# Memory keys and values from plain float32 products, the gating table loaded first, and a new recorded order, in a two-layer encoder trunk on one core

## The chip, the core and the metric

One core of one Trainium2 chip runs the whole program. The metric is the device time of one execution in microseconds; the kernel before has a median of 1061.03 us over three runs (1059.38 to 1061.39). One further execution was taken by the hardware profiler. Every duration below that is not called a median comes from that one.

The engines are named as in the profile: PE (TensorE, matrix products), DVE (VectorE), ACT (ScalarE), POOL (GpSimd), and SP, which issues nearly all the DMAs.

## What is computed

Two layers over a residual stream of 256 tokens by 1024 channels. Each layer is a half-weighted gated feed-forward network, a mixer with an output projection, and a second gated network, with a layer normalization after each. The mixer of layer 0 is a recurrence over time (RWKV-7), that of layer 1 a stick-breaking attention; both also attend to 256 fixed memory tokens, whose keys and values are projected once:

```python
mem_kv = mem @ w_mem_kv                      # (256 x 1024) @ (1024 x 512)
mem_k = split_heads(mem_kv[..., :MEM_WIDTH])
mem_v = split_heads(mem_kv[..., MEM_WIDTH:])
for i in range(DEPTH):
    x = layer_norm(ALPHA * x + 0.5 * swiglu(x, ffn1_w_gate[i], ffn1_w_up[i], ffn1_w_down[i]), ...)
    proj = x @ (rwkv_w_in if i % 2 == 0 else sb_w_in)
    mix = rwkv7_mix(...) or stick_breaking_mix(...)
    heads = concatenate([mix, memory_attention(mq, mem_k, mem_v)])
    x = layer_norm(ALPHA * x + heads @ w_out[i], ...)
    x = layer_norm(ALPHA * x + 0.5 * swiglu(x, ffn2_w_gate[i], ffn2_w_up[i], ffn2_w_down[i]), ...)
```

All arrays are float32. `swiglu` is `(silu(x @ gate) * (x @ up)) @ down`.

## The kernel before

**Tiles.** The 256 tokens are two halves of 128 rows (`hf` 0 and 1). A feed-forward network runs over eleven blocks of 256 hidden channels. For one block and half, PE makes gate and up together (512 columns, eight steps over the 1024 channels), ACT and DVE form the gated product, PE turns it, and PE adds the down products into two accumulation banks of that half.

**Parts.** Most products are not made in float32. A weight piece of 128 x 1024 is loaded into a `raw` buffer; ACT rounds it into `hi` (type float32r) and DVE subtracts, giving the remainder `lo` (`piece`). The moving operand is split in the same way (`split_T`, from a turned tile in PSUM into `xTh`/`xTl` or a `hT` pair), and `mm3` issues three products: hi by hi, hi by lo, lo by hi. The rings hold 11 `raw`, 9 `hi` and 8 `lo` buffers. Where a block is named in `WHOLE`, its down products are plain float32 products of the loaded weights instead, one instruction for three, without ACT and DVE work on the weights.

**Memory.** `memory_kv` loads the two halves of the memory, turns them by PE in two groups of four 128-column blocks, splits each turned group into parts (`mT`, in one `hi` and one `lo` buffer), loads `w_mem_kv` in four pieces of 512 KB, splits each, and makes 8 x 2 x 3 = 48 products of 512 columns into two banks. `mem_attention` reads the results.

**Layer order in time.** The mixer of half 0 runs beside the first network's blocks of half 1; that of half 1 runs beside the second network's blocks of half 0. What follows the last network is the normalization of half 1 and the output. In layer 0 the mixer's end is a chain of small products of 64 x 64 (`Tt`, `Y`, `T`, `L`, `Lm`, `vn`, `Sk`, `S` and so on are its tiles) with DVE and ACT steps between them. This document calls the stretch from its first product out of `Tt` and `Lm` to the first large product after the memory attention the chain; it runs once for each half.

**Tables.** ACT holds one set of function tables. A change of set (Exp, Sigmoid, Ln, Silu; Tanh is in three of them) is one ACT_TABLE_LOAD. `TANH` names blocks whose Silu is made from a Tanh, so that no change is needed, by one more DVE instruction.

**What sets the order.** The program first records every operation as an `Op` in a `Plan`, with a price from `Plan.price`. `Plan.order` then lays them out one by one: of the operations that could start earliest on an engine it takes the one with the smallest priority `pri` (with a charge for a change of table). `Plan.improve` finds the priorities by 60 rounds of backward passes with random shakes and then by 76 seeds (`MOVES`) that shift the priorities of a stretch. On each engine the instructions run in the order laid out; PE, ACT and DVE queues are in order, so an instruction that waits holds up all behind it.

Every operation is issued from one line of `Plan.issue`, so all rows of the profile carry line L636, and a row is told apart by its tiles. A buffer keeps the name of its first user: `raw_20r` is a `raw` buffer whatever it holds, `idle_1r` and `h_33r` hold gated products, `ps_28r` and `ps_29r` are the banks of gate, up and projections, `ps_4r` and `ps_5r` those of turned tiles.

Of the kernel before, what the change touches and what calls it, by code (L numbers as in the profile page):

```python
# [13 lines left out]
F32 = mybir.dt.float32  # L14
F32R = mybir.dt.float32r
I32 = mybir.dt.int32
AF = mybir.ActivationFunctionType
# [4 lines left out]
P = 128  # L22
# [36 lines left out]
TANH = (((0, 1, 2, 3, 4, 8, 9), (1, 2, 3, 5, 9)), ((0, 1, 2, 3, 8, 9), (0, 1, 8)))  # L59
WHOLE = (((1, 2, 4, 5, 6, 9, 10), (0, 1, 2, 4, 5, 6, 7)), ((3,), (1, 6)))  # L60
# [9 lines left out]
ORDERS = ((3, 1, 2, 0), (1, 0, 2, 3), (1, 3, 0, 2), (3, 0, 1, 2))  # L70
FLAGS = dict(t1=False, bt=False, dc=False, out1=False, zl2=False)
# [45 lines left out]
class Engine_:  # L117
# [12 lines left out]
ROUNDS = 60  # L130
SHAKES = (0.0, 100.0, 300.0)
PATIENCE = 8
MOVES = (
# [6 lines left out]
)  # L140
SEED = 5104
TURN = 47040.0


def moved(pri, seed, engines):

    r = random.Random(seed)
    a, width = r.uniform(-2e3, 1.055e6), r.choice((4e3, 1e4, 2e4, 4e4, 1e5))
    sigma, only = r.choice((100.0, 400.0, 1500.0, 4000.0)), r.choice((None, None, None, "PE", "DVE", "ACT", "SP"))
    part, new = r.choice((1.0, 0.3, 0.1, 0.03)), list(pri)  # L150
    for i, x in enumerate(pri):
        if a <= x < a + width and (only is None or engines[i] == only) and r.random() < part:
            new[i] = x + r.gauss(0.0, sigma)
    return new


class Plan:
# [159 lines left out]
    def price(self, o, method, aps, a, k):  # L317
# [11 lines left out]
        elif o.eng == "PE":  # L329
# [4 lines left out]
            if method == "transpose":  # L334
                took, o.lag = 110.0, 175.0
            elif st.dtype == F32R:
                took, o.lag = max(cols / 2.4, m / 1.2) + 13.3, 180.0
            else:
                took, o.lag = 2 * max(cols / 1.2, m / 1.2 + 4), 200.0
                if rows <= 64 and cols > 128:  # L340
                    took *= 1.25
            o.parts.append((took, [(r, c) for r in half(st, rows) for c in half(out, m)], min(rows, P) / P))
        elif o.eng == "ACT":
# [3 lines left out]
            o.took = 95.0 + 0.845 * n + far + 93.0 * ptr + (92.0 if "accum_out" in k else 0.0)  # L347
            o.lag = 95.0
        elif o.eng == "DVE":
# [6 lines left out]
            if sum(free(x) == 1 for x in ins) > 2:  # L356
                o.took += 115.0
# [210 lines left out]
    def improve(self):  # L568

        rng = random.Random(SEED)  # L570
        engines, self.first = [o.eng for o in self.ops], dict(self.groups)
# [3 lines left out]
        for n in range(ROUNDS):  # L575
# [12 lines left out]
            if last[-1] < best[-1]:  # L588
                best, kept, fails = last, (dict(self.buffer), self.groups, last[-2]), 0
                pri = [o.pri for o in self.ops]  # L590
# [4 lines left out]
        if MOVES:  # L595
            for seed in MOVES:
                pri = moved(pri, seed, engines)
            for o in self.ops:
                o.pri = pri[o.i]
            key = lambda i: pri[self.lead[i]] - 4000.0 if i in self.lead else pri[i]  # L600
            self.groups = {k: sorted(g, key=key) for k, g in self.first.items()}
            best = self.order()
            kept = dict(self.buffer), self.groups, best[-2]
# [36 lines left out]
def kernel(ctx, tc, const, x, mem, f1g, f1u, f1d, f2g, f2u, f2d, ln_g, ln_b, w_out, w_mem_kv,  # L640
# [31 lines left out]
    def piece(shape, *srcs, queue=None):  # L672
# [242 lines left out]
    def memory_kv():  # L915
# [5 lines left out]
        for g in range(2):  # L921
# [87 lines left out]
    def rwkv_constants():  # L1009
# [19 lines left out]
        nc.gpsimd.memset(lastc, 0.0)  # L1029
        R.update(gup=gup, rkb=rkb, S=S, lastc=lastc)  # L1030

    def rwkv(hf, res):
# [12 lines left out]
        def shifted(c0, n, *dests):  # L1045

            ch = c0 // P
            ptv = turned(project(hf, rw_in[0], c0, n), 0, n // P)
# [63 lines left out]
        zv = sl("vn", [P, NT, P])  # L1112
        shifted(768, 512, zk[:, 0:4])
        shifted(1280, 512, zk[:, 4:6], zv[:, 0:2])
# [50 lines left out]
        shifted(1792, 512, zv[:, 2:6])  # L1165
# [29 lines left out]
        v = zv.rearrange("p j t -> p (j t)")  # L1195
        V = hv(v)
        hb = hv(sl("g"))
        for g in range(2):
# [78 lines left out]
        for x, view in enumerate(("p i j -> p j i", "p i j -> p i j")):  # L1277
            xv = v4(Xs[x], False)
            nc.copy(xv[:, :, 0:BLK], Tn.rearrange(view), lane[:, 0:1])
            nc.copy(xv[:, :, BLK:], Tn.rearrange(view), lane[:, 1:2])  # L1280

        def put_back(x, scratch, dst, crossed):
# [5 lines left out]
            for b in range(2):  # L1288
                src = sv[:, :, b].rearrange("p s h -> p h s")
                for to, ts, hs in parts:  # L1290
# [44 lines left out]
        for lastl in (False, True):  # L1335
# [16 lines left out]
            for x in (0, 1) if not lastl else (1,):  # L1352
                with nc.together():
                    n = products(six((ac, "tp")), T if x else Y, Y if x else T, 1, 1 - x)
# [8 lines left out]
                if x and not lastl:  # L1363
                    for g in range(2):
                        gs = slice(6 * g, 6 * g + 6)
                        nc.vector.tensor_sub(T[:, gs], T[:, gs], keep[g])
# [248 lines left out]
    nc.gpsimd.memset(idle, 0.0)  # L1615
    bank = ps("acc1")
# [71 lines left out]
```

## Time and profile before

| what | value |
|---|---|
| median of three runs | 1061.03 us |
| the profiled execution, its own time | 1062.11 us |
| span of the instructions in it | 1060.3 us |
| PE busy | 1043.7 us, 98% |
| DVE busy | 879.3 us, 83% |
| ACT busy | 748.0 us, 71% |
| ACT_TABLE_LOAD | 19, 1283 ns each |
| moved by DMA | 303.18 MB, mean 286 GB/s |

The profiled execution is 1.1 us above the median of the runs, and 1.8 us of its time lie outside its span. A matrix product's end is modelled, and products overlap, so the busy time of PE is not the sum of what the products cost; the distance between the starts of two products that follow each other is the better price. A plain float32 product stands as two records in the trace, a product of parts or a turned block as one.

### The profile page before, as it was taken

Reading aid. Unit: us, or ns where it says so; the run is one execution under the profiler, and the core shown is the slowest. Engines: PE = TensorE matmul, PEld = TensorE weight load, DVE = VectorE, ACT = ScalarE, POOL = GpSimd, SP = SyncE. Lnnn points to the kernel's source line nnn. Section 1 sums busy time; section 2 is a strip of 40 time slices with the busy share of each in tenths; the row PEclk is TensorE's granted clock in tenths of the full one; section 3 lists DMA queues with packets and bytes.
Section 4 is the critical chain, followed back from the end, with each engine's and each line's share of the span. In section 5 each row is a group of like instructions: output and inputs, shape, how many; then the busy total and the mean of one; then the engine's idle time right before and its main releaser. Section 6 shows DMA issues by size and latency. Waiting matters only on the chain.

```text
span 1060.3 us, 17884 instructions
## 1 busy us (share of the span) xinstructions
PE 1043.7 (98%) x6275; PEld 836.5 (79%) x6275; DVE 879.3 (83%) x1240; ACT 748.0 (71%) x1067; POOL 5.2 (0%) x20
## 2 busy tenths in 40 slices
PE   8999999999899999999999999999999999999996
PEld 7888888876788766778888888888778777878885
DVE  5776679998999978988799755659899989986796
ACT  6665558967789987667577655547997999676672
POOL 0000000000000000000000000000000000000000
PEclk9999999999899999999999999999999999999998
DMA  9998869778598888899899976758989988998981
GB/s 325 324 368 260 257 197 353 243 235 300 187 300 276 270 282 267 299 329 356 293 330 364 327 231 200 232 169 289 368 297 315 365 287 276 372 366 277 307 279 66
DMA packets 212683, 303.18 MB, mean 286 GB/s; under 512 B 13892, under 2 KB 159728, under 8 KB 212594
## 3 DMA queue, kind: packets, MB, share of 16 engines
q1 hardware_dynamic: 212050, 301.53, 85.6%
q8 instruction: 49, 0.80, 0.3%
q10 hardware_dynamic: 544, 0.52, 0.2%
q14 instruction: 40, 0.33, 0.1%
HBM read 300.95 MB, written 1.05 MB: 285 GB/s over the span
## 4 chain that ended last, share of the span: by engine, by line
PE 94%; ACT 3%; DVE 1%; DMA 1%; issue 0%; ACTq 0%; DVEq 0%; SPq 0%
PE ps_28r L636 28%; PE ps_29r L636 28%; PE ps_24r L636 8%; PE ps_26r L636 8%; PE ps_2r L636 8%; PE ps_25r L636 7%; PE ps_4r L636 3%; PE ps_5r L636 3%; ACT T_338r L636 1%; DMA raw_20r<-in_w_mem_kv_dram 1%; DVE x L636 0%; DMA raw_8r<-in_ffn_w_up_dram 0%; ACT Tt_331r L636 0%; ACT hi_18r L636 0%; ACT bn_383r L636 0%
## 5 line engine op out<-in xcount | busy, mean ns | idle before, releaser
L636 ACT ACTIVATE idle_1r<-ps_29r 128x256 f32<-128x256 f32 (+1 forms) x45 | 19.2, 427 | 27.0 <-PE ps_29r L636 22.2
L636 ACT ACTIVATE h_33r<-ps_28r 128x256 f32<-128x256 f32 (+1 forms) x47 | 19.4, 412 | 24.1 <-PE ps_28r L636 22.8
L636 PE MATMUL ps_28r<-lo_13r,xTh 128*128 128x512 f32 x84 | 32.7, 390 | 0.0
L636 PE MATMUL ps_29r<-lo_13r,xTh 128*128 128x512 f32 x76 | 29.6, 390 | 0.0
L636 ACT ACT_TABLE_LOAD x19 | 24.4, 1283 | 5.8 <-DMA raw_8r<-in_ffn_w_up_dram 5.5
L636 PE MATMUL ps_28r<-lo_40r,xTh 128*128 128x512 f32 (+1 forms) x72 | 27.6, 384 | 0.0
L636 PE MATMUL ps_28r<-lo_43r,xTh 128*128 128x512 f32 (+1 forms) x72 | 27.6, 384 | 0.0
L636 PE MATMUL ps_28r<-hi_15r,xTh 128*128 128x512 f32 (+1 forms) x64 | 26.2, 409 | 0.0
L636 PE MATMUL ps_29r<-lo_22r,xTh 128*128 128x512 f32 x64 | 25.0, 390 | 0.0
L636 PE MATMUL ps_28r<-hi_15r,xTl 128*128 128x512 f32 (+1 forms) x64 | 24.6, 384 | 0.0
L636 PE MATMUL ps_28r<-hi_12r,xTh 128*128 128x512 f32 (+1 forms) x60 | 23.8, 396 | 0.0
L636 PE MATMUL ps_29r<-lo_16r,xTh 128*128 128x512 f32 x60 | 23.4, 390 | 0.0
L636 DVE TENSOR_TENSOR h_33r<-h_33r,ps_28r 128x256 f32<-128x256 f32 x32 | 13.3, 416 | 12.1 <-ACT h_33r L636 12.1
L636 PE MATMUL ps_28r<-hi_12r,xTl 128*128 128x512 f32 (+1 forms) x60 | 23.0, 384 | 0.0
L636 PE MATMUL ps_28r<-hi_6r,xTh 128*128 128x512 f32 x52 | 21.1, 406 | 1.5 <-ACT xTh L636 1.5
L636 PE MATMUL ps_29r<-hi_21r,xTh 128*128 128x512 f32 x56 | 22.4, 401 | 0.0
L636 PE MATMUL ps_29r<-hi_39r,xTh 128*128 128x512 f32 x54 | 22.1, 409 | 0.0
L636 PE MATMUL ps_29r<-hi_21r,xTl 128*128 128x512 f32 x56 | 21.9, 390 | 0.0
L636 PE MATMUL ps_29r<-hi_42r,xTh 128*128 128x512 f32 x52 | 21.6, 416 | 0.0
L636 PE MATMUL ps_28r<-hi_18r,xTh 128*128 128x512 f32 x52 | 21.4, 412 | 0.0
L636 PE MATMUL ps_28r<-hi_45r,xTh 128*128 128x512 f32 (+1 forms) x54 | 21.4, 397 | 0.0
L636 PE MATMUL ps_28r<-hi_6r,xTl 128*128 128x512 f32 x52 | 21.0, 404 | 0.2 <-DVE xTl L636 0.2
(2127 smaller groups left out, 3919.0 us busy)
## 6 DMA issues: line engine op xcount, KB each, us to landing
raw_41r<-in_ffn_w_down_dram SPq DMA_DIRECT2D x17, 512.0 KB, 5.4
raw_11r<-in_ffn_w_gate_dram SPq DMA_DIRECT2D x32, 256.0 KB, 4.5
raw_11r<-in_ffn_w_up_dram SPq DMA_DIRECT2D x32, 256.0 KB, 4.4
raw_14r<-in_ffn_w_gate_dram SPq DMA_DIRECT2D x29, 256.0 KB, 5.0
raw_14r<-in_ffn_w_up_dram SPq DMA_DIRECT2D x29, 256.0 KB, 6.1
raw_23r<-in_ffn_w_gate_dram SPq DMA_DIRECT2D x29, 256.0 KB, 4.5
raw_23r<-in_ffn_w_up_dram SPq DMA_DIRECT2D x29, 256.0 KB, 4.9
raw_53r<-in_ffn_w_down_dram SPq DMA_DIRECT2D x14, 512.0 KB, 6.5
```

The costliest lines, as they stand in the source:

```text
L636: fn(*[at(x) for x in a], **{n: at(x) for n, x in k.items()})
```

## The change

`memory_kv` no longer splits anything. The turned memory is copied as it is into a `raw` buffer, each 512 KB piece of `w_mem_kv` stays in its `raw` buffer, and 16 plain float32 products of 512 columns take the place of the 48. A Silu of one column is issued ahead of all other ACT work, on a tile that POOL clears first; the first rounded weight piece comes behind it. Two blocks of layer 1's second network (3 and 4) join `TANH`; the block numbers 8 and 10 that leave or join the other lists belong to blocks that are not issued through those lists. The order in which `w_out` pieces are used for half 0 of layer 1 is another. `Plan.price` prices ACT, DVE and products a little differently. The search in `improve` is replaced by a stored priority for every operation (`URGENCY`, 147 lines of text that are unpacked into numbers). The flags `pb`, `xt`, `tn` and `vn` are False, so the code behind them isn't issued; it is left out here.

```diff
-TANH = (((0, 1, 2, 3, 4, 8, 9), (1, 2, 3, 5, 9)), ((0, 1, 2, 3, 8, 9), (0, 1, 8)))
-WHOLE = (((1, 2, 4, 5, 6, 9, 10), (0, 1, 2, 4, 5, 6, 7)), ((3,), (1, 6)))
+TANH = (((0, 1, 2, 3, 4, 8, 9), (1, 2, 3, 5, 9)), ((0, 1, 2, 3, 9), (0, 1, 3, 4, 8)))
+WHOLE = (((1, 2, 4, 5, 6, 9, 10), (0, 1, 2, 4, 5, 6, 7)), ((3, 10), (1, 6)))
...
-ORDERS = ((3, 1, 2, 0), (1, 0, 2, 3), (1, 3, 0, 2), (3, 0, 1, 2))
-FLAGS = dict(t1=False, bt=False, dc=False, out1=False, zl2=False)
+ORDERS = ((3, 1, 2, 0), (1, 0, 2, 3), (2, 0, 3, 1), (3, 0, 1, 2))
+FLAGS = dict(t1=False, bt=False, dc=False, out1=False, zl2=False, pb=False, xt=False, mn=True, tn=False, vn=False)
...
-MOVES = (
-    442621, 567911, 487355, 962396, 998421, 729203, 32684, 87830, 416335, 139243, 653452, 651014, 924705, 834835,
...
+URGENCY = (
+    'c-k%8dA!Zl_doD`ZYm{|B9tK!rAUP&nJQBm>O*8`P^5v3p+ts^iDXEIWXhCzo>iz6sZc6HsbnSzXaAn>@BRI8AJ;wS{oZ@+wO+5+daX0a@^_3&GD'
...
@@ Plan.price
-                took, o.lag = max(cols / 2.4, m / 1.2) + 13.3, 180.0
+                took, o.lag = max(cols / 2.4, m / 1.2) + 14.3, 180.0
...
-            o.took = 95.0 + 0.845 * n + far + 93.0 * ptr + (92.0 if "accum_out" in k else 0.0)
-            o.lag = 95.0
+            slow = 250.0 if far and sb(ins[0]) else 0.0
+            o.took = 40.0 + 0.9 * n + slow + 100.0 * ptr + (92.0 if "accum_out" in k else 0.0)
...
@@ Plan.improve
+        if URGENCY:
+            step = np.frombuffer(zlib.decompress(base64.b85decode(URGENCY)), "<i4")
+            for o, p in zip(self.ops, np.cumsum(step)):
+                o.pri = float(p)
...
@@ piece
             firsts.append(nc.scalar.activation(hi[:, part], raw[:, part], AF.Copy))
+            if queue is not None and i == 0:
+                firsts[0].after.append(gating.i)
...
@@ memory_kv
-        for g in range(2):
+        wv = w_mem_kv.rearrange("(k p) c -> p k c", p=P)
+        for g in range(2) if FLAGS["mn"] else ():
+            mT = new(wp, [P, D], F32, "raw", "mT", NRAW).rearrange("p (s k t) -> p s k t", s=NHALF, t=P)
+            for hf, mt in enumerate(rows):
+                nc.copy(mT[:, hf], turned(mt, 4 * g, 4))
+            for q in range(2):
+                w = new(wp, [P, 2, 512], F32, "raw", "raw", NRAW)
+                nc.in_turn("load", nc.sync.dma_start(w, wv[:, 4 * g + 2 * q:4 * g + 2 * q + 2, :]))
+                for j in range(2):
+                    for hf in range(NHALF):
+                        nc.tensor.matmul(o[hf], mT[:, hf, 2 * q + j], w[:, j], start=g + q + j == 0, stop=g + q + j == 3)
+                yield
+        for g in () if FLAGS["mn"] else range(2):
...
     idle = new(tp_, [P, P], F32, "ta", "idle", 2)
     nc.gpsimd.memset(idle, 0.0)
+    gating = nc.scalar.activation(new(tp_, [P, P], F32, "ta", "idle", 2)[:, :1], idle[:, :1], AF.Silu)
```

Counted over the program, PE has 48 products of parts of 512 columns fewer (3678 for 3726) and 16 plain ones of 512 columns more (70 for 54), ACT has 8 roundings fewer (626 for 634), DVE 8 remainders fewer (624 for 632), and ACT 15 table loads for 19. The DMAs are the same in number and size.

Three places show what moves. The first is ACT at the start of the program. In the kernel before:

```order
L636 DMA raw_8r<-in_ffn_w_up_dram 128x2x256
L636 ACT_TABLE_LOAD [waits DMAHW3_49]
L636 ACTIVATE hi_6r<-raw_8r 128x512 [waits DMAHW0_49]
L636 ACTIVATE hi_6r<-raw_8r 128x512
L636 ACTIVATE xTh<-ps_4r 128x4x128 [waits PE_49]
L636 ACTIVATE xTh<-ps_5r 128x4x128 [waits PE_49]
```

In the changed kernel:

```order
L771 DMA raw_9r<-in_ffn_w_up_dram 128x2x256
L771 ACT_TABLE_LOAD
L771 ACTIVATE idle_2r<-idle_1r 128x1 [waits Pool_49]
L771 ACTIVATE hi_7r<-raw_9r 128x512 [waits DMAHW2_49,DMAHW0_49]
L771 ACTIVATE hi_7r<-raw_9r 128x512
L771 ACTIVATE xTh<-ps_5r 128x4x128 [waits PE_49]
L771 ACTIVATE xTh<-ps_6r 128x4x128 [waits PE_49]
```

The table load stood behind the wait for the first weights; now it stands ahead of that wait. The second table load of the kernel before, ahead of the first gated product, is gone.

The second place is PE where the first chain begins. In the kernel before, the six products of parts of one memory step stand ahead of the chain's first small products, and more of them between the small ones:

```order
L636 MATMUL ps_5r<-cst,raw_11r 128x128 x4
L636 MATMUL ps_28r<-hi_6r,hi_15r 128x512
L636 MATMUL ps_28r<-lo_40r,hi_15r 128x512
L636 MATMUL ps_28r<-hi_6r,lo_7r 128x512
L636 MATMUL ps_29r<-hi_6r,hi_15r 128x512
L636 MATMUL ps_29r<-lo_40r,hi_15r 128x512
L636 MATMUL ps_29r<-hi_6r,lo_7r 128x512
L636 MATMUL ps_24r<-Tt_331r,Lm_332r 64x64 x2
```

In the changed kernel, with the turned memory in `raw_24r`:

```order
L771 MATMUL ps_6r<-cst,raw_48r 128x128 x4
L771 MATMUL ps_29r<-raw_51r,raw_24r 128x512 x2
L771 MATMUL ps_5r<-cst,raw_15r 128x128 x4
L771 MATMUL ps_6r<-cst,raw_48r 128x128 x4
L771 MATMUL ps_30r<-raw_51r,raw_24r 128x512
L771 MATMUL ps_27r<-raw_9r,hT_487r 128x512
L771 MATMUL ps_25r<-Tt_332r,Lm_333r 64x64 x2
```

Three of the 16 plain products stand ahead of the chain's first small products, and 13 between them.

The third place is DVE just ahead of the chain's first additions into `Tt`. In the kernel before:

```order
L636 TENSOR_TENSOR lo_43r<-raw_53r,hi_45r 128x1024
L636 TENSOR_TENSOR lo_7r<-ps_5r,hi_15r 128x512
L636 TENSOR_TENSOR lo_7r<-ps_4r,hi_15r 128x512
L636 SCALAR_TENSOR_TENSOR x_79<-x_79,ps_2r 128x512
L636 SCALAR_TENSOR_TENSOR x_79<-x_79,ps_26r 128x512
L636 TENSOR_TENSOR lb_435r<-lb_435r,g_426r 128x768
L636 TENSOR_TENSOR lo_13r<-raw_14r,hi_39r 128x1024
L636 TENSOR_TENSOR lo_19r<-ps_5r,hi_18r 128x512
L636 TENSOR_TENSOR lo_22r<-raw_44r,hi_42r 128x1024
L636 BN_STATS st_572r<-x_79 128x6 x2
L636 TENSOR_TENSOR Tt_331r<-Tt_331r,ps_24r 128x384
```

In the changed kernel:

```order
L771 COPY raw_24r<-ps_5r 128x512
L771 TENSOR_SCALAR Tt_332r<-Y_340r,cst 128x12x16
L771 TENSOR_TENSOR lb_436r<-lb_436r,g_427r 128x768
L771 SCALAR_TENSOR_TENSOR x_79<-x_79,ps_27r 128x512
L771 BN_STATS st_573r<-x_79 128x6
L771 TENSOR_TENSOR Tt_332r<-Tt_332r,ps_6r 128x384
```

The remainders of the memory weights and of the turned memory are gone; one of the four copies of the turned memory stands on DVE, and three on ACT. The remainders for the products behind the chain (`lo_20r` and the following) now stand inside the chain.

More of the change, by code (lines that the diff above doesn't have):

```diff
@@ L1 @@
+import base64
 import heapq
@@ L3 @@
 import random
+import zlib
 from contextlib import contextmanager
@@ L140 @@
 )
-SEED = 5104
+SEED = 53017
 TURN = 47040.0
[L145 to L154, printed above, removed]
@@ L1163, in rwkv @@
         yield "p4"
-        shifted(1792, 512, zv[:, 2:6])
+        if FLAGS["vn"]:
+            shifted(1792, 512, apart=(0, own[:, 256:]))
+            nc.sync.dma_start(ago[1:P], own[:P - 1])
+            if hf == 0:
+                nc.gpsimd.memset(ago[0:1], 0.0)
+            for q in range(4):
+                there, here = R["row"][q:q + 1], slice(192 * q, 192 * q + 192)
+                if hf == 0:
+                    nc.sync.dma_start(there, own[P - 1:P, here])
+                else:
+                    nc.sync.dma_start(ago[0:1, here], there)
+        else:
+            shifted(1792, 512, zv[:, 2:6])
         if hf == 0:
```

243 lines of the change are left out of this document (218 added, 25 removed), and 5 rows, old and new, of the table MOVES.

## The prediction, made before the changed kernel was run

> **What bounds the kernel now.** I read the page's busy times and slices first, then the busy times by stage, then who waits for whom, and last the rows of single instructions. The page:
>
> ```profile
> PE 1043.7 (98%) x6275; PEld 836.5 (79%) x6275; DVE 879.3 (83%) x1240; ACT 748.0 (71%) x1067; POOL 5.2 (0%) x20
> PE   8999999999899999999999999999999999999996
> DVE  5776679998999978988799755659899989986796
> PEclk9999999999899999999999999999999999999998
> ```
>
> PE is the bound nearly everywhere, and its clock is whole but for a dip in slice 11. So the time is PE's work plus PE's waits, and a change pays where it takes from one of the two. By stage (columns: stretch, its length, then busy time of PE, PEld, DVE, ACT and POOL, granted clock, DMA share, GB/s):
>
> ```profile
> 6.03:9.45 3.42, 1.66 (x10) 1.01 (x9) 1.97 (x4) 3.41 (x6) 0.00 (x0) 1.00 1.09 367
> 9.45:12.86 3.41, 3.41 (x8) 2.73 (x9) 3.41 (x4) 2.32 (x3) 0.00 (x0) 0.50 1.07 398
> 151.80:302.90 151.10, 146.70 (x1393) 115.70 (x1392) 142.45 (x248) 119.24 (x210) 2.58 (x7) 0.98 0.78 263
> 250.70:286.80 36.10, 32.44 (x672) 25.36 (x671) 32.82 (x64) 25.59 (x51) 1.64 (x5) 0.91 0.78 262
> 279.10:285.90 6.80, 5.84 (x75) 4.71 (x65) 6.46 (x21) 4.46 (x11) 0.00 (x0) 0.50 0.47 139
> 302.90:448.80 145.90, 145.29 (x1366) 109.47 (x1365) 133.08 (x226) 120.95 (x202) 1.21 (x3) 1.00 0.85 278
> 393.60:426.00 32.40, 32.40 (x648) 22.69 (x648) 25.45 (x34) 24.68 (x38) 0.26 (x1) 1.00 0.80 266
> 440.00:1000.00 560.00, 560.00 (x2655) 453.46 (x2655) 465.20 (x591) 396.35 (x514) 0.00 (x0) 1.00 0.91 303
> ```
>
> From 440 to 1000 us PE has no idle time: nothing is to be won there, and any wait that the new order makes is paid in full. Stage one (151.8 to 302.9, between the first normalizations of the two mixers' ends) holds the first chain, at 250.7 to 286.8. There PE idles 151.1 - 146.7 = 4.4 us, and from 279.1 to 285.9 its clock is 0.50, so 5.84 us of its work would have taken 2.9: 7.3 us of loss that the rows show. DVE is busy 142.45 of 151.1 us in the same stage, 94%; it is the engine that PE waits behind. Stage two (302.9 to 448.8) idles 0.6 us, its chain (393.6 to 426.0) none.
>
> **The start.** The loss lies at one place:
>
> ```profile
> 5.52 1.28 ACT L636 ACT_TABLE_LOAD   x1 [5.52 <-DMA raw_8r<-in_ffn_w_up_dram]
> 6.82 1.15 ACT L636 ACTIVATE hi_6r<-raw_8r 128x512 fp32r<-128x512 f32 x2
> 7.87 0.58 ACT L636 ACTIVATE xTh<-ps_4r 128x512 fp32r<-128x512 f32 x1
> 8.50 0.50 PE L636 MATMUL ps_28r<-hi_6r,xTh 128*128 128x512 f32 x1 [1.48 <-ACT xTh L636]
> 10.45 0.63 PE L636 MATMUL ps_28r<-lo_7r,xTh 128*128 128x512 f32 x1
> 10.87 0.63 PE L636 MATMUL ps_28r<-hi_6r,xTl 128*128 128x512 f32 x1
> 13.41 0.39 PE L636 MATMUL ps_28r<-hi_12r,xTh 128*128 128x512 f32 x1
> 13.64 0.39 PE L636 MATMUL ps_28r<-lo_13r,xTh 128*128 128x512 f32 x1
> 16.98 1.28 ACT L636 ACT_TABLE_LOAD   x1
> ```
>
> The table load waits for the first weights although it needs none; behind it the rounding, the turned x and PE's first large product follow without a gap. With the load ahead of the wait, it runs while the DMA flies (ACT idles 5.52 us), and the chain to 8.50 shortens by its 1.28 us: -1.3, with the weights' own landing as the new limit, since hi_7r waits for it as before. Bounds -1.3 and 0, should x or its turning come last instead (the first x piece now loads ahead of the constants). The second load at 16.98 goes too; PE had no gap there, so nothing for it.
>
> After that start the clock is 0.50 from 9.45 to 12.86, and products stand 0.42 us apart instead of 0.23. Eight products (x8) thus lose 8 x 0.2 = 1.6 us. The low stretch follows one in which PE was busy 1.66 of 3.42 us; 1.3 us more of busy time there would make 2.9. Whether that keeps the clock no row tells, so I take half, -0.8, bounds 0 and -1.6. [...]
>
> **The memory products.** PE's price, from the distance of starts:
>
> ```profile
> 926.32 1.02 PE L636 MATMUL ps_25r<-raw_14r,hT_2111r 128*128 128x512 f32 x2
> 927.18 1.02 PE L636 MATMUL ps_24r<-raw_14r,hT_2111r 128*128 128x512 f32 x2
> ```
>
> A plain product takes 0.86 us, three of parts 3 x 0.227 = 0.68 (0.23 apart at 13.41 above). 16 plain for 48 of parts: 13.7 - 10.9 = **+2.8 us** of PE work, on the engine that bounds. [...]
>
> What DVE and ACT no longer do:
>
> ```profile
> 241.76 1.18 DVE L636 TENSOR_TENSOR lo_40r<-raw_20r,hi_6r 128x1024 fp32r<-128x1024 f32 x1
> 248.01 0.68 DVE L636 TENSOR_TENSOR lo_7r<-ps_5r,hi_15r 128x512 fp32r<-128x512 f32 x1
> 248.61 0.68 DVE L636 TENSOR_TENSOR lo_7r<-ps_4r,hi_15r 128x512 fp32r<-128x512 f32 x1
> 1028.12 1.22 DVE L636 TENSOR_TENSOR lo_43r<-raw_44r,hi_9r 128x1024 fp32r<-128x1024 f32 x1
> 1029.26 1.22 DVE L636 TENSOR_TENSOR lo_7r<-raw_53r,hi_6r 128x1024 fp32r<-128x1024 f32 x1
> 253.08 1.06 ACT L636 ACTIVATE hi_12r<-raw_47r 128x1024 fp32r<-128x1024 f32 x1
> 254.02 1.06 ACT L636 ACTIVATE hi_9r<-raw_20r 128x1024 fp32r<-128x1024 f32 x1
> 231.83 8.73 DMA raw_20r<-in_w_mem_kv_dram
> ```
>
> Four remainders of weights at 1.14 us from start to start and four of turned memory at 0.60 are 7.0 us off DVE, less one copy of 0.6 that it takes over; four roundings at 0.94 are 3.8 us off ACT. All of it lies just ahead of the chain or in it, where DVE is at 94%. The last row, from the chain that ended last, shows the weights' DMA holding that path for 8.73 us; the path now leads from the DMA straight to PE.
>
> ```profile
> PE ps_24r L636 <- ACT Lm_332r L636: 1.8, 1, 1.8
> PE ps_4r L636 <- DVE S_112r L636: 0.9, 1, 0.9
> PE ps_5r L636 <- DVE lo_7r L636: 0.7, 1, 0.7
> PE ps_26r L636 <- ACT Tt_331r L636: 0.6, 1, 0.6
> ```
>
> These are PE's waits in the chain: for ACT and DVE steps, one of them for a remainder of the turned memory itself. Freed of 7.0 us, DVE reaches the chain's additions earlier, and it still works ahead: in the new order seven remainders for the products behind the chain stand before its end, in the old one eight. I count 60% of the 4.4 us of idle time as won, 2.6, and the 2.9 of the clock, since it fell where PE idled most: **-5.5 us**. Bounds: -7.3 (all that the rows show; DVE's relief of 7.0 is about as much) and 0, if the chain's own steps and not DVE's load set its pace.
>
> **The rest of the order.** The new priorities move every stage. For stage two I take -1: its idle 0.6 and a little of the spacing of its small products. Bounds: -4 (ACT and DVE are busy 76% and 79% of the chain's 32.4 us, so it has room to be a tenth shorter, 3.2, and the idle 0.6 can go) and +4, about the 4.4 us that stage one idles now. From 440 us on I take 0, bounds 0 and +4, by the same row. There two blocks more use Tanh, which removes two table loads and adds two DVE instructions, beside a PE without idle time: nothing. The plain down products of block 10 do not come to be, since the count of plain products rises by the memory's 16 alone. Behind the last product nothing changes:
>
> ```profile
> 1049.40 0.69 DVE L636 SCALAR_TENSOR_TENSOR x<-x,ps_26r 128x512 f32<-128x512 f32 x1 [2.59 <-PE ps_26r L636]
> ```
>
> From here the normalization's same DVE steps and the output follow, 10.9 us to the span's end.
>
> **Sum.** -1.3 - 0.8 + 2.8 - 5.5 - 1.0 = -5.8 us. The profiled execution took 1062.1 us (span 1060.3); with the change 1056.3. It stood 1.1 above the median of the runs, so I forecast a median of 1055 us.
>
> **Rivals.** (1) *A much better order.* All 7.3 us of stage one go, stage two gives 4, the clock at the start stays whole: -1.3 - 1.6 + 2.8 - 7.3 - 4 = -11.4, 1049.6. [...] Against it: the chain is a row of dependent steps, and fewer DVE instructions do not shorten any of them. 20%.
>
> (2) *The waits only move.* DVE's load was not what held the chain; then the 5.5 of the memory part and stage two's 1 fall away: -1.3 - 0.8 + 2.8 = +0.7, 1061.7. For it: of the four waits only one is for a remainder. 15%, of which 8 within what can be told from no change.
>
> (3) *The weight buffers run short: slower.* The two memory halves, two turned groups and four weight pieces now stay in `raw` until PE has used them, eight of 11 buffers, and PE uses the last of them in the middle of the chain. Loads for the output projection behind the chain then start late. If the first of them has not begun to fly when the chain ends, PE waits for one load,
>
> ```profile
> raw_11r<-in_ffn_w_gate_dram SPq DMA_DIRECT2D x32, 256.0 KB, 4.5
> raw_41r<-in_ffn_w_down_dram SPq DMA_DIRECT2D x17, 512.0 KB, 5.4
> ```
>
> 5.4 us for 512 KB, with nothing won in the chain: -1.3 - 0.8 + 2.8 + 5.4 = +6.1, 1067. For it: PE consumes in order, so one late piece stops all. Against it: seven remainders for those products stand in DVE's order ahead of the chain's end, hence their loads too. 15%.
>
> My forecast keeps 50%.
>
> **Numbers.** About 0.2%, 2.1 us, is what a measurement here tells from no change: 1058.9 to 1063.2. The forecast and rival 1 lie below it, 70% together; rival 2 gives 8% within, 2% below and 5% above; rival 3 lies above, 15%. So faster 0.72, same 0.08, slower 0.20. The forecast's own range, by its bounds taken together, is 1050 to 1059. The range that should hold the time 8 times in 10 reaches into rival 1 and to rival 3: 1044 to 1066.
>
> **What would show it.** Right: ACT's first table load ends before 5 us and PE's first large product starts near 7.2 us; the chain from the first product out of `Tt` to the first large product after it takes some 31 us instead of 36.1, with no stretch at clock 0.50 in it; 16 plain products stand 0.86 us apart or are split by chain products; DVE's busy time falls by some 4 to 7 us. Wrong: idle time of PE after 440 us; a wait of PE for a `raw` buffer of `w_mem_kv` or `w_out`; a chain as long as before.

## The result, and the profile after

The changed kernel takes 1063.86 us (median of six runs, 1063.45 to 1065.24), the old one beside it 1060.99 us (six runs). The ratio is 1.0034, with a 95% interval of 1.0024 to 1.0044: slower by 2.5 to 4.7 us. The forecast was 1055 us; the result lies inside the predicted range and on the other side of no change. In what follows a ratio is turned into microseconds by 1061 us, so 0.1% is 1.06 us.

The page of the changed kernel, busy times:

```profile
PE 1044.2 (98%) x6259; PEld 832.6 (78%) x6259; DVE 882.3 (83%) x1239; ACT 737.8 (69%) x1055; POOL 5.2 (0%) x20
PEclk9999999999899999999999999999999999999999
```

PE is the bound as before, and the dip of its clock in slice 11 is still there. By stage (columns as in the prediction: stretch, its length, busy time of PE, PEld, DVE, ACT and POOL, granted clock, DMA share, GB/s):

```profile
150.20:300.90 150.70, 146.50 (x1364) 110.85 (x1363) 132.99 (x235) 112.92 (x201) 2.58 (x7) 0.97 0.76 253
249.02:287.78 38.76, 34.56 (x653) 23.15 (x653) 28.27 (x56) 24.64 (x48) 1.64 (x5) 0.87 0.77 264
...
277.40:287.64 10.24, 8.14 (x129) 6.98 (x125) 8.66 (x20) 6.37 (x14) 0.45 (x2) 0.50 0.50 155
443.00:1003.00 560.00, 560.00 (x2659) 454.26 (x2658) 469.51 (x591) 393.30 (x512) 0.00 (x0) 1.00 0.90 302
403.20:435.10 31.90, 28.73 (x632) 19.74 (x631) 23.05 (x31) 20.60 (x34) 0.26 (x1) 1.00 0.86 277
```

The first row is the stretch that corresponds to stage one. DVE did get the relief: 133.0 us busy where it was 142.5. PE did not: it idles 150.7 - 146.5 = 4.2 us, where it idled 4.4. The chain (second row, from its first product to the first large product behind the memory attention) takes 38.8 us instead of 36.1, and the stretch at clock 0.50 in it has grown from 6.8 to 10.2 us. The second chain (last row) had no idle time and now has 31.90 - 28.73 = 3.2 us. From 443 to 1003 us PE is busy throughout, as before.

The start, on ACT, from the timeline (start, duration, instruction, idle time before it and what ended it):

```profile
1.75 1.28 ACT L771 ACT_TABLE_LOAD   x1 [1.75 <-issue]
3.04 0.20 ACT L771 ACTIVATE idle_2r<-idle_1r 128x1 f32<-128x1 f32 x1
5.51 1.15 ACT L771 ACTIVATE hi_7r<-raw_9r 128x512 fp32r<-128x512 f32 x2 [2.27 <-DMA raw_9r<-in_ffn_w_up_dram]
```

The load has moved under the flight of the weights, and the first rounding starts as soon as they land, at 5.51. PE's rows there:

```profile
6.69 0.66 PE L771 MATMUL ps_6r<-cst,x 128*128 128x128 f32 x4 [1.18 <-DMA x<-in_x_dram]
7.19 0.39 PE L771 MATMUL ps_3r<-idle_1r 128*128 128x128 f32 x2
7.33 0.48 PE L771 MATMUL ps_29r<-hi_7r,xTh 128*128 128x512 f32 x1
```

The first large product starts at 7.33 instead of 8.50, and now x is what PE waits for, 1.18 us. The low clock from 9.45 to 12.86 is not in this profile.

The plain products of the memory part (x2 is one product, two records; the view that the last row is from ends inside its second product, hence x3):

```profile
258.63 1.02 PE L771 MATMUL ps_29r<-raw_67r,raw_18r 128*128 128x512 f32 x2
259.49 1.88 PE L771 MATMUL ps_29r<-raw_21r,raw_18r 128*128 128x512 f32 x4
261.21 1.45 PE L771 MATMUL ps_30r<-raw_67r,raw_18r 128*128 128x512 f32 x3
```

One takes 259.49 - 258.63 = 0.86 us, the next two (261.21 - 259.49) / 2 = 0.86: the price that the sum used.

PE's waits in the whole execution (who waits for whom: total, times, longest):

```profile
PE ps_6r L771 <- issue: 3.2, 1, 3.2
PE ps_5r L771 <- DVE L_345r L771: 1.7, 1, 1.7
PE ps_6r L771 <- DMA x<-in_x_dram: 1.2, 1, 1.2
PE ps_26r L771 <- ACT Lm_333r L771: 1.1, 1, 1.1
PE ps_5r L771 <- DVE S_113r L771: 1.0, 1, 1.0
```

The waits for `L`, `Lm` and `S` are for steps of the chain itself. The longest of all is for "issue": the profile shows nothing that PE waited for. The old kernel has one such wait, of 0.9 us, in the first chain. This one lies in the second chain, inside a block of 24 products:

```profile
411.86 0.21 PE L771 MATMUL ps_6r<-Tt_332r,Lm_333r 64*64 64x64 f32 x1 [3.17 <-issue]
```

So three things had to be explained: why DVE's relief left PE's idle time as it was, what the plain products really cost, and what the new wait is.

### The profile page after: what moved, and what is told of

Its sections match the earlier page's. It is cut to its first block, busy times and chain, and to the rows that moved or that the text cites. A ratio compares the mean times of both kernels' runs of the same rounds, so it can differ in the third digit from the quotient of the medians.

```text
span 1063.4 us, 17788 instructions
## 1 busy us (share of the span) xinstructions
PE 1044.2 (98%) x6259; PEld 832.6 (78%) x6259; DVE 882.3 (83%) x1239; ACT 737.8 (69%) x1055; POOL 5.2 (0%) x20
## 4 chain that ended last, share of the span: by engine, by line
PE 97%; DVE 1%; DMA 1%; issue 0%; ACT 0%; SPq 0%; DVEq 0%; ACTq 0%
PE ps_29r L771 30%; PE ps_30r L771 28%; PE ps_27r L771 8%; PE ps_26r L771 8%; PE ps_3r L771 8%; PE ps_25r L771 8%; PE ps_6r L771 4%; PE ps_5r L771 3%; DMA raw_12r<-in_ffn_w_up_dram 1%; DVE x L771 0%; DVE lo_11r L771 0%; SPq L771 0%; DVE S_113r L771 0%; ACT hi_10r L771 0%; DVE L_345r L771 0%
## 5 line engine op out<-in xcount | busy, mean ns | idle before, releaser
L771 PE MATMUL ps_30r<-lo_44r,xTh 128*128 128x512 f32 x76 | 29.6, 390 | 0.0
L771 PE MATMUL ps_29r<-lo_14r,xTh 128*128 128x512 f32 (+1 forms) x72 | 27.2, 378 | 0.0
L771 PE MATMUL ps_30r<-hi_13r,xTh 128*128 128x512 f32 x60 | 23.7, 394 | 0.0
L771 PE MATMUL ps_29r<-hi_16r,xTh 128*128 128x512 f32 (+1 forms) x60 | 23.6, 394 | 0.0
L771 PE MATMUL ps_30r<-hi_13r,xTl 128*128 128x512 f32 x60 | 23.4, 390 | 0.0
L771 PE MATMUL ps_30r<-lo_8r,xTh 128*128 128x512 f32 x60 | 23.4, 390 | 0.0
L771 PE MATMUL ps_30r<-lo_41r,xTh 128*128 128x512 f32 x60 | 23.4, 390 | 0.0
L771 PE MATMUL ps_30r<-hi_16r,xTh 128*128 128x512 f32 x58 | 23.1, 398 | 0.0
L771 PE MATMUL ps_29r<-lo_44r,xTh 128*128 128x512 f32 (+1 forms) x60 | 23.0, 383 | 0.0
L771 PE MATMUL ps_29r<-hi_16r,xTl 128*128 128x512 f32 (+1 forms) x60 | 23.0, 383 | 0.0
```

Of the source, the lines that this page charges most:

```text
L771: fn(*[at(x) for x in a], **{n: at(x) for n, x in k.items()})
```

## The experiments

Unless said otherwise an experiment keeps the order of the kernel that it starts from, instruction by instruction; the order was written out as a list in place of the priorities. "Chain" lengths are read as above, from one profiled execution each; the mean clock, the granted clock of PE over a whole execution, is recorded for every execution. All results together (us is the ratio less 1, by 1061 us):

| kernel | median, us | ratio to the old kernel, 95% interval | us |
|---|---|---|---|
| changed kernel | 1063.86 | 1.0034 (1.0024 to 1.0044) | +3.6 |
| e1: old, early table load | 1058.65 | 0.9985 (0.9976 to 0.9993) | -1.6 |
| e2: old, no memory remainders | 1059.68 | 0.9991 (0.9983 to 1.0000) | -1.0 |
| e3: old, plain memory | 1064.81 | 1.0043 (1.0029 to 1.0057) | +4.6 |
| e4: changed, rows shifted | 1072.68 | 1.0111 (1.0095 to 1.0127) | +11.8 |
| e5: changed, dense run spread | 1064.19 | 1.0035 (1.0022 to 1.0048) | +3.7 |
| e6: changed, chain kept busy | 1061.27 | 1.0008 (0.9999 to 1.0017) | +0.8 |
| e7: old, both edits | 1063.06 | 1.0026 (1.0015 to 1.0038) | +2.8 |
| e8: changed, memory of parts | 1062.82 | 1.0030 (1.0019 to 1.0042) | +3.2 |
| e9: old, chain kept busy | 1060.22 | 0.9999 (0.9990 to 1.0008) | -0.1 |
| e10: old, early load, kept busy | 1058.36 | 0.9982 (0.9974 to 0.9991) | -1.9 |
| e11: changed, parts, kept busy | 1064.03 | 1.0031 (1.0020 to 1.0042) | +3.3 |
| e12: changed, spread, kept busy | 1062.98 | 1.0020 (1.0011 to 1.0028) | +2.1 |

**e1: the early table load alone.**

```diff
     nc.gpsimd.memset(idle, 0.0)
+    gating = nc.scalar.activation(new(tp_, [P, P], F32, "ta", "idle", 2)[:, :1], idle[:, :1], AF.Silu)
...
             firsts.append(nc.scalar.activation(hi[:, part], raw[:, part], AF.Copy))
+            if queue is not None and i == 0:
+                firsts[0].after.append(gating.i)
```

> The old kernel and its order, with one Silu of one column ahead of all other ACT work and the first rounding behind it; nothing else differs. If the start of the program is set by the table load (1.28 us) between the weights' landing and their rounding, the time falls by 1.3 to 1.5 us against the old kernel, and the first large product starts at about 7.2 us instead of 8.5. Rival: x or its turning comes last instead; then less than 0.5 us.

Measured: -1.6 us (-2.5 to -0.7). The start is worth what the table load lasts, within the interval. This kernel is faster than both the old and the changed one.

**e2: DVE's relief alone.** The products of the memory part stay, and only the remainders go (`l` is `h` here, the rounded piece):

```diff
-                to_T(mt[:, g * 512:(g + 1) * 512], [t[:, hf] for t in mT], 0, 4)
+                to_T(mt[:, g * 512:(g + 1) * 512], (mT[:, hf], None), 0, 4)
...
-                    mm3(o[hf], mT[0][:, hf, k % 4], mT[1][:, hf, k % 4], h, l, k == 0, k == KT - 1)
+                    mm3(o[hf], mT[:, hf, k % 4], mT[:, hf, k % 4], h, l, k == 0, k == KT - 1)
```

> The old kernel and its order, but the eight remainders of the memory part (7.0 us of DVE) are left out; the 48 products stay, each reading the rounded part where it read a remainder, so memory keys and values are less exact. PE and ACT have the same work. Theory of the prediction, that DVE's load holds the first chain: the chain takes 31 to 33 us instead of 36.1 and the time falls by 3 to 7 us. Rival, that the chain's own row of dependent steps sets its pace: chain 35 to 37 us, time within 1 us of the old kernel.

(The keys and values are three times too large here, since a triple adds the same product three times.) Measured: -1.0 us (-1.8 to 0.0). The chain took 33.5 us, which by itself is neither what the theory expected (31 to 33) nor what the rival did (35 to 37). The comparison has to be with e1, whose profiled execution also had a whole clock there. The chain's row of e1:

```profile
248.87:283.63 34.76, 29.92 (x672) 23.21 (x671) 31.90 (x62) 25.28 (x51) 1.64 (x5) 1.00 0.81 271
```

and of e2:

```profile
248.70:282.21 33.51, 29.58 (x671) 23.04 (x671) 28.23 (x58) 25.65 (x51) 1.63 (x5) 1.00 0.81 273
```

DVE has 3.7 us less to do in it, and the chain is 1.25 us shorter. Where that comes from is in PE's waits from 245 to 290 us. e1:

```profile
PE ps_25r L696 <- ACT Lm_333r L696: 1.8, 1, 1.8
PE ps_5r L696 <- DVE S_113r L696: 1.4, 1, 1.4
PE ps_25r L696 <- issue: 0.9, 1, 0.9
PE ps_6r L696 <- DVE lo_8r L696: 0.4, 1, 0.4
```

e2:

```profile
PE ps_24r L696 <- ACT Lm_332r L696: 1.8, 1, 1.8
PE ps_5r L696 <- DVE S_112r L696: 1.4, 1, 1.4
PE ps_5r L696 <- ACT eT_604r L696: 0.4, 1, 0.4
```

The two waits for the chain's own steps are the same, 1.8 and 1.4; the blocks in which they lie take 2.70 and 1.97 us in both (from the first product of `L,Tt` to the rest of `Lm,RB`, and `Lm,bn`). What went is the wait for "issue" inside a block `Tt,Lm`, which took 2.09 us in e1 and 0.86 in e2: with that the 1.25 us are accounted for. Ahead of the chain there went the wait of 0.4 us for a remainder of the memory part itself. No dependent step came earlier because DVE had less to do. The relief did not shorten the chain's waits; the prediction's reason for -5.5 us falls here. (e2's profiled execution, at 1057.59 us, is the fastest of its eleven, and the others have a lower mean clock, 0.994 to 0.996 for 0.998, so it is compared with e1's profile and not taken for an average.)

**e3: the plain products alone**, by the diff of `memory_kv` shown ahead of the prediction, in the old order.

> The old kernel and its order, with the memory part made of plain products as in the changed kernel; no early table load. Three loads of the output projection and their roundings stand a little later, since raw buffers are taken. The price of PE alone is 16 x 0.86 - 48 x 0.227 = 2.8 us. If DVE's relief pays as predicted (-5.5), the time falls by 2.7 us; if it pays nothing, the time rises by 2 to 4 us; if the raw buffers run short as in the rival of the prediction, by 5 or more, with a wait of PE behind the chain.

Measured: +4.6 us (+3.1 to +6.0), so 1.8 us more than PE's own price of 2.8. The chain:

```profile
250.58:290.44 39.86, 35.47 (x657) 22.84 (x657) 28.68 (x60) 25.18 (x50) 1.64 (x5) 0.91 0.74 259
```

It is 3.8 us longer than the old one (36.10, with 32.44 of PE and the same clock of 0.91): 3.0 us are PE's, 0.7 are idle time. PE's waits from 262 to 292 us have three that the old kernel does not have, 1.6 us in sum:

```profile
PE ps_5r L696 <- ACT Lm_332r L696: 0.7, 1, 0.7
PE ps_4r L696 <- ACT idle_1r L696: 0.7, 1, 0.7
...
PE ps_4r L696 <- ACT Lm_332r L696: 0.2, 1, 0.2
```

ACT's timeline says why it was late with `Lm`:

```profile
269.20 1.06 ACT L696 ACTIVATE hi_39r<-raw_8r 128x1024 fp32r<-128x1024 f32 x1 [2.17 <-DMA raw_8r<-in_w_out_dram]
270.17 0.47 ACT L696 ACTIVATE Lm_332r<-ps_5r 64x384 f32<-64x384 f32 x1
```

ACT stood 2.17 us before a rounding of a `w_out` piece whose load came late, and the copy of `Lm` that PE needed was queued behind it. The load stands in SP's queue behind one that waited for `raw_47r`, which holds the turned memory: SP's longest wait there, 9.3 us, is for PE and ends at 260.45, with PE's last product out of that buffer; the load of `raw_8r` is issued at 261.90. This is the shortage of the third rival, smaller than priced, and it reaches PE through ACT's queue, not by a product that lacks its weights. (The place of the late loads in the list was chosen for this experiment; in the changed kernel ACT has no wait for a DMA from 267.6 to 284 us.) It need not be all of the 1.8: in return the old kernel's waits for a remainder and for "issue" are gone from this profile, and every profile with plain memory and no idle products has 6.8 to 10.2 us of half clock in the chain, while of the three with parts in the old order (the old kernel's, e1, e2) only the first has any. Which of the two makes up the rest was not settled; e7 below has two executions with a mean clock of 0.998, in which no such stretch has room, and they took 1062.50 and 1062.55 us, so the half clock is hardly all of it.

**e4: PE's stream of instructions shifted.**

```diff
-    warm(WARM[0])
+    warm(2)
+    for _ in range(51):
+        nc.tensor.matmul(bank[:HD, :HD], idle[:HD, :HD], idle[:HD, :HD], start=True, stop=True)
```

> The changed kernel and its order, but seven of the nine idle products at the start are replaced by 51 idle products of 64x64 that take about as long. PE's stream of instructions is 176 rows longer there, and everything behind stands 176 rows later in it. In the trace the transfers of queue 'instruction' move 16 KB for every 256 rows of PE, and the 3.4 us stall at 408.5 ends just after one of them that began 3.4 us late. Theory, that PE ran out of instructions there: the stall moves off the dense run, no stall above 1.5 us at 405 to 415, and the time falls by 2 to 3.4 us. Rival, that a semaphore or a buffer holds that product: stall and time stay as in the changed kernel.

The time, +11.8 us, does not answer the question: 51 small products that all write the same place took 0.2 us each, and the first large product came 8 us late. But behind the start the kernel is the changed one, row for row, and its second chain shows what was asked. Durations of blocks (start to start, from the two traces):

```
block          changed kernel   e4
T,Y   x24           1.34       1.34
Tt,Lm x24           4.25       0.85
two plain           1.91       1.92
Y,T   x24           0.86       1.59
vn,Sk x24           0.86       0.86
vn,Sk x24 (2nd)     0.81       1.26
L,Tt  x12           0.85       0.84
Lm,bn x12           0.46       1.92
```

The stall has left its block and turned up, in three pieces, at blocks that had none; every other block is the same to 0.01 us. In e4's timeline:

```profile
419.62 0.21 PE L693 MATMUL ps_27r<-Y_340r,T_339r 64*64 64x64 f32 x1 [0.42 <-issue]
425.36 0.27 PE L693 MATMUL ps_27r<-vn_314r,Sk_344r 64*64 64x64 f32 x2 [0.18 <-issue]
432.27 0.21 PE L693 MATMUL ps_6r<-Lm_333r,bn_384r 64*64 64x64 f32 x1 [1.26 <-issue]
```

No semaphore and no buffer moves with the count of rows; the supply of instructions would. So the wait for "issue" is PE without instructions. The page of the changed kernel has one queue for PE's (packets, MB, share of 16 engines' time):

```profile
q8 instruction: 49, 0.80, 0.3%
```

and its DMA view, from 405.9 to 409.3 us (the first row) and from 409.3 to 410.5 (the other two):

```profile
q1 hardware_dynamic: 774, 1.23, 99.6%
...
q1 hardware_dynamic: 367, 0.41, 94.6%
q8 instruction: 1, 0.02, 5.3%
```

49 transfers of 16 KB serve 2 x 6259 rows of products and weight loads, some 256 rows each. The one that ended the wait flew only at 409.39, behind data at a share of 99.6%; the one before it had flown at 387.75. Counted from the trace (all rows of PE: products, weight loads and some 60 semaphore and drain rows), PE went through 514 rows between the two, and stood still. The same count can be made for every wait of PE for "issue" in the profiles of all fourteen kernels. There are fifteen of them, 0.2 to 3.2 us long. Each began after exactly 449 + 256 k rows of the kernel, with k the number of transfers before the one that ended it, and ended 1.3 to 1.5 us after that one had landed: the old kernel's 0.9 us at 3009 rows (k 10), the changed kernel's 3.2 us at 5825 (k 21), the three of e4 at 6081, 6337 and 6593 (k 22, 23 and 24). A semaphore or a buffer would not keep to such a count.

**e5: the dense run spread.** PE's moves, by operation (the block that each now stands behind):

```diff
+ behind T,Y:    four plain products (two raw,eT and two raw,hT)
+ behind Tt,Lm:  gup,zl and three products of parts
+ behind vn,Sk:  three products of parts
+ behind 2nd vn,Sk, L,Tt and Lm,bn: one plain, three of parts, one plain and three of parts
```

> The changed kernel with ten products of its second chain moved forward on PE: four plain products of 0.86 us stand between the blocks Y,T / T,Y and the next Tt,Lm, which in the changed kernel followed without a gap; the others close the places that they left. No work is added or removed. Theory, that PE ran out of instructions in that dense run (4.25 us for a block that takes 0.86): the block takes under 1.5 us, and the time falls by 1.5 to 3.4 us against the changed kernel, to 1060.5 to 1062.4. Rival, that the chain's dependent steps need this time anyway: the wait turns up at a later block and the time stays within 1 us of 1063.9.

Measured: +3.7 us, the changed kernel's +3.6. The block `Tt,Lm` took 0.86 us, as the theory had it, but the next `vn,Sk` took 0.8 us longer (the profile has 0.6 of it as a wait for DVE's step into `Tt`), and `L,Tt` and `vn,kn` took 0.4 us longer each behind steps that were no longer covered. The rival was right about the time. One of the five executions, with a mean clock of 0.997, took 1061.77 us; the other four, at 0.992 to 0.995, took 1064.00 to 1064.68.

**e6: PE kept busy in the first chain.**

```diff
+    spare = ps("gu")
+    for _ in range(4):
+        nc.tensor.matmul(spare, ident, cst[:, :512], start=True, stop=True)
```

> The changed kernel with four idle plain products of 512 columns put into the three gaps of PE in the first chain (two at 274.7, one at 277.3, one at 280.5), so that PE is busy there. In the profile of the changed kernel 10.2 us of that chain have clock 0.50. If this half clock is what makes the chain long, no row of it has clock 0.50 and the time falls by 2 to 4 us, to 1060 to 1062. Rival, that ACT's and DVE's steps set its pace: the clock is whole, and the time is within 1 us of the changed kernel or up to 1.5 us above, for idle products that stand in front of a step that is ready.

Measured: +0.8 us (-0.1 to +1.8), 2.8 us less than the changed kernel, by adding work. The chain:

```profile
248.68:285.55 36.87, 35.20 (x662) 21.48 (x661) 27.64 (x54) 24.44 (x48) 1.64 (x5) 1.00 0.83 277
```

The clock is whole and the chain 1.9 us shorter (38.76 before). In this execution the wait for "issue" in the second chain was 1.1 us instead of 3.2, so the profile's gain is not the half clock's alone. In all eleven executions the mean clock is 0.997 or 0.998; in the six of the changed kernel it is 0.993 to 0.996.

**e7: both edits in the old order.**

> The old kernel's order with both edits, the early table load and the plain memory products: everything of the change but its order. If the two measured parts add up (-1.8 and +4.4), 1063.0 us. The new order is then worth the difference to the changed kernel's 1063.9: a new order that wins what the prediction counted for it (1 us in stage two and more) would leave this kernel at 1065 or above; an order that wins nothing leaves it at 1062 to 1064.

Measured: +2.8 us (+1.6 to +4.0); e1 and e3 add to -1.6 + 4.6 = +3.0. The parts add up, and the new order (with the Tanh blocks and the order of the `w_out` pieces, which e7 leaves as they were) is worth +3.6 - 2.8 = +0.8 us, which the intervals do not tell from nothing.

**e8: the changed kernel's order with memory made of parts** (`mn=False`, with the eight roundings and remainders put into the list).

> The changed kernel and its order with the memory part made from parts again: 48 products in the places of the 16, eight roundings and eight remainders (7 us of DVE) put in some 3 to 4.5 us ahead of the first product that reads them. If plain products cost only their PE time, 2.8 us less than the changed kernel, 1061; if they cost what they cost in the old order (4.4), 1059.5; if the relief of DVE was needed by the new order, 1064 or more, with waits of PE for remainders or for DVE's steps in the first chain.

Measured: +3.2 us (+2.0 to +4.5). Between this and the changed kernel no difference can be told. It is no clean price: the remainders put in by hand brought a wait of their own (PE for `lo_44r`, 1.1 us).

**e9 and e10: the old chain kept busy**, without and with the early table load; three idle products, two ahead of `Lm,RB` and one behind `Lm,bn`.

> The old kernel and its order with three idle plain products of 512 columns in the two long gaps of PE in the first chain (two ahead of Lm,RB at 276.2, one behind Lm,bn at 280.0). The prediction counted 2.9 us of the old chain's loss as half clock. If the half clock costs that, the chain has clock 1.00 and the time falls by 2 to 3 us; if the gaps between dependent steps would stand there at any clock, it falls by less than 1 us or rises by up to 1.

> The same three idle products, with the early table load as well. The early load alone gave 1058.65 us, and its profiled execution had no half clock in the chain. [...]

Measured: e9 -0.1 us (-1.1 to +0.8), e10 -1.9 us (-2.8 to -1.0), 0.3 from e1. The chain of e9 has a whole clock:

```profile
250.35:285.31 34.96, 32.84 (x677) 24.21 (x677) 31.91 (x62) 25.29 (x51) 1.64 (x5) 1.00 0.81 269
```

So taking the half clock away by three more products wins nothing that can be measured. That is not yet the price of the half clock, for these products, 0.86 us each, stand on PE too. The old kernel's own executions, timed beside e1 to e12 in four sets, say more: of 80, the 38 with a mean clock of 0.994 or less have a median of 1061.1 us, the 29 with 0.996 or more 1059.9, and in each set the first are 0.7 to 1.4 us slower. So low clock, that at the start included, goes with about 1.2 us; which is the cause of the other is not shown. e10 is the fastest kernel of the study, not told apart from e1.

**e11: e8 with the chain kept busy.**

> The changed kernel's order with the memory part made from parts (1062.8 without more) and the four idle products in the first chain's gaps (1061.3 with plain products). If the half clock is what the new order's chain loses, whatever memory is made of, 1059.5 to 1060.5; if the 7 us of DVE work come to matter once the clock is whole, 1062 or more.

Measured: +3.3 us (+2.1 to +4.5), as e8. Its profiled execution, the slowest of its seven (1066.74; the fastest 1062.40), had waits for instructions in both chains:

```profile
PE ps_26r L693 <- issue: 2.6, 1, 2.6
PE ps_3r L693 <- issue: 2.3, 1, 2.3
```

Both ended with a transfer; PE had gone through 503 and 520 rows since the one before.

**e12: spread and kept busy together.**

> The changed kernel with both repairs: the four idle products in the first chain's gaps (1061.3 us alone), and PE's dense runs broken in both chains (1064.2 with the second chain's alone): one memory product stands between Tt,Lm and T,Y of the first chain, and the moves of the run with four plain products between the second chain's blocks. No stall inside a block of 24 or 12 products should exceed 1 us. If running out of instructions costs the changed kernel its stalls in most executions, the two gains add: 1058.5 to 1060. If the 3.4 us of the one profiled execution were chance, or the chain gives the time back, 1061 to 1062, as with the idle products alone.

Measured: +2.1 us (+1.2 to +3.0), 1.3 more than e6. Its profile has a whole clock, and the one wait for instructions left is short:

```profile
PE ps_5r L693 <- DVE S_113r L693: 1.0, 1, 1.0
PE ps_5r L693 <- DVE Tt_332r L693: 0.6, 1, 0.6
PE ps_30r L693 <- issue: 0.4, 1, 0.4
```

The gains did not add. The reading that fits e5 and e12 is that products moved into the dense run delay the chain and leave later steps bare, and that this costs as much as the missing instructions did.

## Why the prediction was wrong, point by point

**The bound.** That PE bounds the program, and that the second half leaves nothing to win or lose, was right: 560.00 of 560.00 us busy before and after.

**The start, -2.1.** Right: -1.6 (e1), with the interval from -2.5 to -0.7. The prediction's other case, that x would come last, is what the trace shows, and the first large product still starts 1.17 us earlier. The half of the clock's 1.6 us that it added was a guess: none of the ten profiles with the early load has that low stretch, and three of the four without it do (e2 does not), but its price was not measured by itself.

**The memory products, +2.8.** Right as PE's price, 0.86 us a product. As the price of the edit in the old order it was too small: +4.6. Of the 1.8 more, part are waits for ACT behind a late load (e3), and part may be the half clock. What it costs in the changed order e8 could not settle.

**Stage one, -5.5.** This is the step that failed: "it is the engine that PE waits behind" took DVE's 94% for a cause. The prediction also read its four waits wrongly. Of those "in the chain" only `Lm` (1.8 us) and `S` (0.9) lie there; the one for the remainder `lo_7r` ends at 248.75, ahead of the chain, and the one for `Tt` lies in stage two. The third wait in the old chain is one that it left out:

```profile
PE ps_24r L636 <- issue: 0.9, 1, 0.9
```

So no wait in the chain was for a remainder. The relief came, 9.5 us of DVE's time in that stage, and PE's idle time there went from 4.4 to 4.2 us. Alone, in the old order, it was worth 1.0 us (0.0 to 1.8, e2), and not by any step of the chain. There the chain's two long waits stayed at 1.8 and 1.4 us, as in e1; in the changed kernel the wait for `L` is 1.7 us, and the timelines show what stands behind it. ACT:

```profile
275.00 0.48 ACT L771 ACTIVATE Y_340r<-ps_5r 64x384 f32<-64x384 f32 x1 [0.74 <-PE ps_5r L771]
```

DVE:

```profile
275.51 0.56 DVE L771 TENSOR_TENSOR L_345r<-L_345r,ps_5r 64x384 f32<-64x384 f32 x1 [0.41 <-ACT Y_340r L771]
275.99 0.55 DVE L771 TENSOR_TENSOR L_345r<-L_345r,ps_6r 64x384 f32<-64x384 f32 x1
```

ACT idles until PE's products are there, DVE idles until ACT has copied `Y`, and PE idles until DVE has added to `L`, at 276.6. At this place none of the three is busy with something else, so other work taken off one of them frees nothing here. The prediction said as much itself, against the first rival, and gave the other reading 50%.

**The half clock, 2.9 of that -5.5.** It did not go with DVE's relief: the stretch grew to 10.2 us. Nor was it worth 2.9 in the old order, where e9 took it away and won 0.1 us (-0.8 to +1.1), and executions with a low clock are about 1.2 us slower than those with a high one. In the changed order it seems to cost more: e6 won 2.8 us, and within e5 the one execution with a high clock was 2.2 us or more faster; the changed kernel's own six executions, from 0.993 to 0.996, show no such trend.

**Stage two, -1.** Wrong in sign in the profiled execution, within the stated bound of +4: PE lost 3.2 us there to a wait that neither the prediction nor its rivals had. How much of it an average execution pays stays open: from profile to profile the longest such wait ran from 0.4 us (e12) to 3.2, and the moves that shortened it (e5, e12) gave the time back elsewhere.

**The range.** The forecast's own range, 1050 to 1059, is not what its bounds give together. The lower ones add up to -11.4, 1050; the upper ones, 0 + 0 + 2.8 + 0 + 4 + 4, to +10.8, 1072.

**The rivals.** The second, "the waits only move", had the mechanism; its +0.7 lacked 1.8 us for the plain products in the old order and whatever the new order added. The third, the shortage of buffers, showed itself in e3 through ACT.

**The sum as it came out**, from runs: -1.6 (table load) + 4.6 (plain products in the old order) - 0.2 (both together, against their sum) + 0.8 (new order) = +3.6 us. Only the first of its parts was worth keeping: alone (e1), it makes the kernel faster.

## What to carry to other kernels

A busy share of 94% does not make an engine the one that is waited behind; look at the single waits, follow each to its releaser, and ask whether the releaser itself was idle just before. If it was, do not count on relief for it: here it was (DVE, for 0.41 us ahead of its step into `L`), and 3.7 us less work for DVE in the chain (e2) left the two long waits at 1.8 and 1.4 us. An edit that gives work to the bounding engine is paid there (here 2.8 of the 4.6 us, an estimate from 0.86 and 0.227 us a product), and the buffers that it holds longer can make a later load late for whoever is queued behind it (2.17 us of ACT in e3).

## What was unexpected of the hardware

- PE ran out of instructions. A transfer of 16 KB went with some 256 rows and took about 1.0 us (0.88 to 1.50 in the changed kernel), but in the two chains some came too late, beside data at a DMA share of 95 to 100% where that was looked at (the changed kernel and e11). Blocks of 24 products of 64x64 use 96 rows in 0.86 us, so the 256 rows of one transfer last for 256 / 96 = 2.7 of them, 2.3 us (an estimate from these figures). The profiles have fifteen stalls of 0.2 to 3.2 us, called "issue", each after 449 + 256 k rows, and moved by shifting the rows (e4).
- The half clock differs between executions of one program, and between programs: the first chain has a stretch of 6.83 us at clock 0.50 in the old kernel's profile and of 10.24 us in the changed kernel's, the old kernel's start one of 3.41 us, and there is none in the chain of e1 and e2 (clock 1.00), which has the long gaps of the old one (waits of 1.8 and 1.4 us); the mean clock of the old kernel's executions runs from 0.992 to 0.998.
- Small products that all write the same place of PSUM took 0.2 us each at the start of the program (e4), against 0.86 / 24 = 0.036 us in the chain's blocks, which go to two places by turns. Whether the one place or the start of the program makes the difference is not shown.
